# The second convolution's first DFT step: through DRAM instead of SBUF, with the jobs, the load buffers and the moves regrouped

## Chip, cores and metric

One core of a Trainium2 chip. The metric is the device time of one execution in microseconds (us); the median of several runs counts.

## What is computed

One layer of a diffusion trunk on 2048 tokens of width 1024: a modulated norm, a Hyena long convolution of order 2, a residual norm, and an expert-choice mixture of 16 SwiGLU experts. The change lies in the long convolution alone. The reference, cut to it:

```python
def _hyena(h, w_in, b_in, conv_w, conv_b, ..., f_bias, w_out, b_out):
    u = _centred_conv3(h @ w_in + b_in, conv_w, conv_b)
    v, x1, x2 = jnp.split(u, 3, -1)
    kf = _hyena_filters(L, ...)                 # rfft of two filters per channel
    def long_conv(zin, o):
        zf = zin.astype(F32)
        y = jnp.fft.irfft(jnp.fft.rfft(zf, n=2 * L, axis=1) * kf[None, :, o], n=2 * L, axis=1)[:, :L]
        return (y + zf * f_bias[o].astype(F32)).astype(h.dtype)
    z = x1 * long_conv(v, 0)
    z = x2 * long_conv(z, 1)
    return z @ w_out + b_out
```

So there are two long convolutions in a row per channel. The gated result of the first (order 0) is the input of the second (order 1).

## The kernel before

`phase_conv` does both convolutions. The 1024 channels are cut into four channel blocks `cb` of 256, and a *job* is one channel block and one order `o`: eight jobs, in the order cb 0 and 1 with o = 0, cb 0 and 1 with o = 1, then the same for cb 2 and 3. I number them 0 to 7; "a second-order job" is one with o = 1.

A transform of 4096 points is done as two DFT steps, both matmuls with constant matrices. The result of the first step for the first product (`ud`), and the transformed filters after their first step (`fud`), were written to DRAM by earlier stages. A job runs over 16 groups `gp`. For each group it

- loads a filter tile `kr` (from `fud`) and an input tile `xr`; a tile of 512 KB covers two groups (`fetch_k` L825, `fetch` L815 and L819);
- does the second DFT step of both on PE into `xp` (`spec` L833, `fwd` L853), copies the filter's spectrum with ACT, and multiplies the spectra on DVE (L858, L859);
- does the first step of the inverse on PE (`inv`, `ap`), copied by ACT to `ao` (L872), and moves it in two DMAs of 128 KB from `ao` into a tile `bn`, which regroups the partitions (`put`, L879).

While job j runs, its groups 2 to 9 also finish job j - 1: `bst` does the inverse's second step on PE from `bn` into `sb`, for order 0 in three passes on operands that `bsplit` split into a high part (ACT, L900) and a low part (POOL, L901); `gate` multiplies by x1 or x2 (DVE, L929). After an order 1 product the gated result goes to DRAM (`zd`, L937). After an order 0 one it is split (ACT L933, POOL L934), and `s1st` does the second product's first DFT step on it at groups 4 to 11: three-pass matmuls into `sb`, copied by ACT (L806) into tiles `s1o` in SBUF. The second-order job two places later gets its `xr` from `s1o`, by DMAs of 128 KB from SBUF to SBUF, two per group.

The order is written out by hand: every engine works off its instructions in the order in which the loop below issues them, and DMAs go out in order from the queue of the engine that issues them. SP issues all loads and the first of the two moves of a group, POOL the second. `ahead` sends `kr` five groups ahead and `xr` four, each with two buffers. `after` starts the next stage's weights (`wod`) during the last job.

Of the kernel before, what the change touches and what calls it, by code (L numbers as in the profile page):

```python
# [12 lines left out]
F32 = mybir.dt.float32  # L13
# [28 lines left out]
AH = 2  # L42
SB = 3
# [70 lines left out]
def host_consts():  # L114
    f4 = np.float32
    S1, S2, A, B = dft_mats()
    c = {}
# [4 lines left out]
    c["c_s1p"] = S1.transpose(1, 0, 2)[:, :, spread]  # L122
# [647 lines left out]
def phase_conv(tc, A, wst, s2, am, fud, ud, x1d, x2d, zd, O, after):  # L770
# [4 lines left out]
    with ExitStack() as st:  # L775
# [6 lines left out]
        so = rst.enter_context(tc.tile_pool(reuse_waits="tile", name="c_so", bufs=3, side="right"))  # L782
# [7 lines left out]
        nc.sync.dma_start(s1, A["c_s1p"])  # L790
# [3 lines left out]
        jobs = [(2 * b2 + b, o) for b2 in range(2) for o in range(2) for b in range(2)]  # L794
        s1o, bn, kk, kr, xr = {}, {}, {}, {}, {}
# [3 lines left out]
        def s1st(j, q):  # L799
            if q == 0:  # L800
                s1o[j] = [so.tile([128, 16, 256], F32, name="s1o") for _ in range(2)]
            zh, zl = zs.pop((j, q))
            for th in range(2):
                p = ps.tile([128, 2, 256], F32, name="sb", bufs=3)
                mm3(nc, p, s1h[:, th], s1l[:, th], zh, zl)
                nc.scalar.copy(s1o[j][th][:, 2 * q:2 * q + 2], p)  # L806

        def fetch(j, gp):
            cb, o = jobs[j]
            th = gp // 8  # L810
            gl = (2 * gp) % 16
            if gp % 2 == 0:
                r = rt.tile([128, 4, 256], F32, name="xr", bufs=2)
                if o == 0:
                    nc.sync.dma_start(r, ud[cb, th, gl:gl + 4].rearrange("g p c -> p g c"))  # L815
                xr[j, gp], xr[j, gp + 1] = r[:, 0:2], r[:, 2:4]
            if o == 1:
                for i in range(2):
                    nc.sync.dma_start(xr[j, gp][:, i], rows8(s1o[j][th], gl + i))  # L819

        def fetch_k(j, gp):
            cb, o = jobs[j]
# [97 lines left out]
        def gate(j, q, p):  # L920
# [9 lines left out]
            if o == 0:  # L930
# [4 lines left out]
                zs[j + 2, q] = zh, zl  # L935
# [5 lines left out]
        def ahead(n):  # L941
            for d, f in ((AH + 3, fetch_k), (AH + 2, fetch), (AH + 1, spec), (AH, fwd)):
                m = n + d
                if 0 <= m < len(order) and (d != AH + 3 or m % 2 == 0):
                    f(*order[m])

        for n in range(-AH - 3, 0):
            ahead(n)
        for n, (j, gp) in enumerate(order):
# [10 lines left out]
            if (j + 1, q) in zs:  # L960
                s1st(j + 1, q)
# [717 lines left out]
def build(tc, A, out):  # L1679
    nc = tc.nc  # L1680
    with ExitStack() as st:
# [3 lines left out]
        ud = dr.tile([4, 2, 16, 128, 256], F32, name="ud")  # L1685
        x1d = dr.tile([4, 128, 16, 256], F32, name="x1d")
# [59 lines left out]
        phase_conv(tc, A, wst, S.s2, S.am, fud, ud, x1d, x2d, zd, O, lambda w4, wk: out_start(tc, A, wst, w4, wk, wod, zd, rowd, O))  # L1746
# [20 lines left out]
```

## Time and profile before

| | |
|---|---|
| time, three runs | 4205.91, 4205.35, 4202.3 us; median 4205.35 |
| the profiled execution | 4207.69 us, span 4205.7 us |
| mean granted PE clock | 0.967 of full |
| busy share of the span | PE 93%, DVE 62%, ACT 45%, POOL 23% |
| the convolution, first to last copy `ao` | 1037.3 to 1610.6 us |

The span is what the profiler's trace covers; the rows further down are from this one execution. Most of the kernel is the expert stage behind the convolution, with PE at 90% and more. The convolution's 573 us are a seventh of the span.

### The profile page before, as it was taken

The page shows a single profiled execution, that of the slowest core. Times are in us where ns is not written, and L with a number is a line of the kernel's source. Part 1 is how long each engine was busy: PE and PEld are TensorE (multiplying, and loading weights), DVE is VectorE, ACT ScalarE, POOL GpSimd, SP SyncE. Part 2 cuts the span into 40 slices and gives each one's busy share as a digit, 9 for nine tenths or more (in the row PEclk, how much of TensorE's full clock was granted, in tenths as well). Part 3 has the DMA queues.
Part 4 walks back from the last instruction along what each step waited for, and adds up shares of the span by engine and source line. Part 5 has one row for each costly group of instructions (what it writes and reads, how often), then busy time and mean ns, then how long its engine had stood idle before and what let it go on. Part 6 is the DMA issues. An engine that isn't in the chain of part 4 may idle for free.

```text
span 4205.7 us, 59336 instructions
## 1 busy us (share of the span) xinstructions
PE 3916.2 (93%) x23158; PEld 3360.2 (80%) x23158; DVE 2623.2 (62%) x3636; ACT 1886.3 (45%) x2609; POOL 961.1 (23%) x918
## 2 busy tenths in 40 slices
PE   6788999999998987965999999999999999999997
PEld 2445787787777776755999999999999999998996
DVE  7997444776766766876555555555555555556666
ACT  4554332334876873122444444444444444444443
POOL 4674211222332342120000000000000000005635
PEclk7999999999999999987999999999999999999999
DMA  6665445666778776543566666666566656656664
GB/s 188 189 203 177 129 153 174 206 212 194 208 208 230 208 222 205 166 165 123 189 213 201 191 190 201 200 191 201 192 209 194 204 193 209 193 171 228 225 230 166
DMA packets 648180, 815.30 MB, mean 194 GB/s; under 512 B 51411, under 2 KB 543203, under 8 KB 645596
## 3 DMA queue, kind: packets, MB, share of 16 engines
q1 hardware_dynamic: 593442, 694.82, 52.3%
q0 software_dynamic: 37472, 113.86, 9.3%
q10 hardware_dynamic: 16986, 2.83, 0.4%
q8 instruction: 182, 2.98, 0.3%
q14 instruction: 98, 0.80, 0.1%
HBM read 627.04 MB, written 133.97 MB: 181 GB/s over the span
## 4 chain that ended last, share of the span: by engine, by line
PE 74%; DVE 10%; DMA 8%; issue 4%; POOL 3%; ACT 1%; SPq 0%; POOLq 0%; DVEq 0%; ACTq 0%
PE ab L175 10%; PE ab L177 10%; PE ab L176 10%; PE acc L175 5%; PE acc L176 5%; PE acc L177 5%; PE ip L175 4%; PE ip L177 4%; PE ip L176 4%; DMA xr<-s1o 3%; PE xp L853 1%; PE op L175 1%; PE op L177 1%; PE op L176 1%; PE xp L833 1%
## 5 line engine op out<-in xcount | busy, mean ns | idle before, releaser
L177 PE MATMUL ab<-xh,w1l 128*128 128x256 f32 x2048 | 581.5, 284 | 3.2 <-DVE w1l L1386 3.0
L175 PE MATMUL ab<-xh,w1h 128*128 128x256 f32 x2048 | 582.9, 285 | 0.0
L177 PE MATMUL ab<-xh,w3l 128*128 128x256 f32 x2048 | 579.7, 283 | 0.5 <-DVE w3l L1386 0.5
L176 PE MATMUL ab<-xl,w1h 128*128 128x256 f32 x2048 | 579.8, 283 | 0.0
L176 PE MATMUL ab<-xl,w3h 128*128 128x256 f32 x2048 | 579.6, 283 | 0.0
L175 PE MATMUL ab<-xh,w3h 128*128 128x256 f32 x2048 | 579.6, 283 | 0.0
L1386 DVE TENSOR_TENSOR w2l<-w2r,w2h 128x2048 fp32r<-128x2048 f32 x126 | 297.6, 2362 | 317.6 <-ACT w2h L1385 317.6
L175 PE MATMUL acc<-w2h,hh 128*128 128x512 f32 x1024 | 405.4, 396 | 14.0 <-ACT hh L170 13.5
L176 PE MATMUL acc<-w2l,hh 128*128 128x512 f32 x1024 | 403.3, 394 | 0.0
L177 PE MATMUL acc<-w2h,hl 128*128 128x512 f32 x1024 | 400.5, 391 | 0.8 <-DVE hl L171 0.8
L175 PEld LDWEIGHTS ab<-xh,w1h 128*128 128x128 f32 x2048 | 392.5, 192 | 8.8 <-ACT xh L1469 0.3
L176 PEld LDWEIGHTS ab<-xl,w1h 128*128 128x128 f32 x2048 | 392.4, 192 | 8.6
L177 PEld LDWEIGHTS ab<-xh,w1l 128*128 128x128 f32 x2048 | 392.2, 191 | 4.2 <-DVE w1l L1386 4.2
L177 PEld LDWEIGHTS ab<-xh,w3l 128*128 128x128 f32 x2048 | 393.2, 192 | 0.9 <-DVE w3l L1386 0.9
L176 PEld LDWEIGHTS ab<-xl,w3h 128*128 128x128 f32 x2048 | 393.2, 192 | 0.0
L175 PEld LDWEIGHTS ab<-xh,w3h 128*128 128x128 f32 x2048 | 393.1, 192 | 0.0
L1492 DVE TENSOR_TENSOR s<-s,ab 128x256 f32<-128x256 f32 x256 | 106.9, 417 | 399.6 <-ACT s L1491 399.5
L1386 DVE TENSOR_TENSOR w1l<-w1r,w1h 128x2048 fp32r<-128x2048 f32 x126 | 301.0, 2389 | 69.5 <-ACT w1h L1385 69.4
L1386 DVE TENSOR_TENSOR w3l<-w3r,w3h 128x2048 fp32r<-128x2048 f32 x126 | 292.9, 2325 | 53.8 <-ACT w3h L1385 53.8
L1515 POOL DMA_INDIRECT accd<-y,idx x27 | 64.4, 2385 | 1120.2 <-DVE y L1509 1120.2
L1385 ACT CAST w2h<-w2r 128x2048 fp32r<-128x2048 f32 x128 | 244.0, 1906 | 153.3 <-PE acc L177 145.1
L1491 ACT ACTIVATE s<-ab 128x256 f32<-128x256 f32 x256 | 97.4, 380 | 448.0 <-PE ab L177 448.0
(401 smaller groups left out, 8728.1 us busy)
## 6 DMA issues: line engine op xcount, KB each, us to landing
w1r<-in_moe_w_dram SPq DMA_DIRECT2D x128, 1024.0 KB
w3r<-in_moe_w_dram SPq DMA_DIRECT2D x128, 1024.0 KB
w2r<-in_moe_w_dram SPq DMA_DIRECT2D x128, 1024.0 KB
fud<-ev SPq DMA_DIRECT2D x128, 256.0 KB
kr<-fud SPq DMA_DIRECT2D x64, 512.0 KB
mw<-in_mod_w_dram SPq DMA_DIRECT2D x96, 256.0 KB
wraw<-in_hy_w_in_dram SPq DMA_DIRECT2D x48, 512.0 KB
win<-in_c_win_dram SPq DMA_DIRECT2D x64, 256.0 KB
```

The source lines that it names most:

```text
L175: nc.tensor.matmul(out, lhsT=ah, rhs=bh, start=start, stop=False)
L176: nc.tensor.matmul(out, lhsT=ah, rhs=bl, start=False, stop=False)
L177: nc.tensor.matmul(out, lhsT=al, rhs=bh, start=False, stop=stop)
L833: nc.tensor.matmul(p[:, i], lhsT=s2[:, 2 * gp + i], rhs=r[:, i], start=True, stop=True)
L853: nc.tensor.matmul(p[:, i], lhsT=s2[:, 2 * gp + i], rhs=r[:, i], start=True, stop=True)
L1385: nc.scalar.copy(h, raw)
L1386: eng.tensor_tensor(l, raw, f_(h), OP.subtract)
L1491: nc.scalar.activation(s, p[:, 0], AF.Silu)
L1492: nc.vector.tensor_tensor(s, s, p[:, 1], OP.mult)
L1515: nc.gpsimd.indirect_dma_start(out=accd, out_offset=at(idx, h), in_=y, in_offset=None, compute_op=OP.add)
```

## The change

The jobs run in the order o = 0 for all four channel blocks, then o = 1 for all four. The first DFT step's result is copied by ACT into a small tile `s1t` (three buffers of 256 KB) instead of `s1o`, and written from there to a new DRAM tile `z1d`, in the layout of `ud`, by a DMA on POOL's queue. A second-order job loads `xr` from `z1d` as a first-order one does from `ud`: one DMA of 512 KB for two groups. `kr` and `xr` have four buffers each and are sent eight to nine groups ahead. Both moves of a group go on POOL's queue (those of the last four groups on SP's and ACT's). Even jobs' second `bn` tile has a place of its own, `bn2`. The constant of the first step is no longer permuted (`c_s1` for `c_s1p`).

```diff
-        so = rst.enter_context(tc.tile_pool(reuse_waits="tile", name="c_so", bufs=3, side="right"))
...
-        jobs = [(2 * b2 + b, o) for b2 in range(2) for o in range(2) for b in range(2)]
+        jobs = [(cb, o) for o in range(2) for cb in range(4)]
...
         def s1st(j, q):
-            if q == 0:
-                s1o[j] = [so.tile([128, 16, 256], F32, name="s1o") for _ in range(2)]
             zh, zl = zs.pop((j, q))
             for th in range(2):
                 p = ps.tile([128, 2, 256], F32, name="sb", bufs=3)
                 mm3(nc, p, s1h[:, th], s1l[:, th], zh, zl)
-                nc.scalar.copy(s1o[j][th][:, 2 * q:2 * q + 2], p)
+                t = rt.tile([128, 2, 256], F32, name="s1t", bufs=3)
+                nc.scalar.copy(t, p)
+                nc.gpsimd.dma_start(z1d[jobs[j][0], th].rearrange("g (s n) c -> (g s) n c", s=8)[:, 2 * q:2 * q + 2], t)

         def fetch(j, gp):
             cb, o = jobs[j]
-            th = gp // 8
             gl = (2 * gp) % 16
-            if gp % 2 == 0:
-                r = rt.tile([128, 4, 256], F32, name="xr", bufs=2)
-                if o == 0:
-                    nc.sync.dma_start(r, ud[cb, th, gl:gl + 4].rearrange("g p c -> p g c"))
-                xr[j, gp], xr[j, gp + 1] = r[:, 0:2], r[:, 2:4]
-            if o == 1:
-                for i in range(2):
-                    nc.sync.dma_start(xr[j, gp][:, i], rows8(s1o[j][th], gl + i))
+            r = rt.tile([128, 4, 256], F32, name="xr", bufs=XR)
+            nc.sync.dma_start(r, (ud, z1d)[o][cb, gp // 8, gl:gl + 4].rearrange("g p c -> p g c"))
+            xr[j, gp], xr[j, gp + 1] = r[:, 0:2], r[:, 2:4]
...
-            r = rt.tile([128, 4, 256], F32, name="kr", bufs=2)
+            r = rt.tile([128, 4, 256], F32, name="kr", bufs=XR)
...
-                bn.setdefault(j, []).append(wk.tile([128, 16, 256], F32, name="bn", bufs=3))
+                own = th and j % 2 == 0
+                bn.setdefault(j, []).append((rt if own else wk).tile([128, 16, 256], F32, name="bn2" if own else "bn", bufs=1 if own else 3))
...
-                (nc.sync, late and nc.scalar or nc.gpsimd)[i].dma_start(rows8(bn[j][gp // 8], gl), ao[:, i])
+                (late and (nc.sync, nc.scalar)[i] or nc.gpsimd).dma_start(rows8(bn[j][gp // 8], gl), ao[:, i])
...
-                zs[j + 2, q] = zh, zl
+                zs[j + 4, q] = zh, zl
...
-            for d, f in ((AH + 3, fetch_k), (AH + 2, fetch), (AH + 1, spec), (AH, fwd)):
+            for d, f in ((AH + 2 * XR - 1, fetch_k), (AH + 2 * XR - 2, fetch), (AH + 1, spec), (AH, fwd)):
                 m = n + d
-                if 0 <= m < len(order) and (d != AH + 3 or m % 2 == 0):
+                if 0 <= m < len(order) and (d < AH + 2 or m % 2 == 0):
                     f(*order[m])
...
-            if (j + 1, q) in zs:
-                s1st(j + 1, q)
+            if (j + 3, q) in zs:
+                s1st(j + 3, q)
```

POOL's order in job 1, at the last group without and the first with a split and a first DFT step, before:

```order
L934 TENSOR_TENSOR w<-z,w 128x512
L879 DMA bn<-ao 8x16x256
L934 TENSOR_TENSOR w<-z,w 128x512
L901 TENSOR_TENSOR w<-bn,w 128x512 x2
L879 DMA bn<-ao 8x16x256
```

The full groups after the change (`bn_8886` is `bn2`):

```order
L929 TENSOR_TENSOR w<-z,w 128x512
L896 TENSOR_TENSOR w<-bn,w 128x512
L896 TENSOR_TENSOR w<-bn_8886,w 128x512
L806 DMA z1d<-s1t 128x512 x2
L874 DMA bn<-ao 8x16x256 x2
L929 TENSOR_TENSOR w<-z,w 128x512
```

A group's round on POOL now holds two writes to `z1d` and two moves where it held one move; they stand between the splits of one group and the low part (L929) of the next.

SP's order where the first second-order job's loads go out, before:

```order
L825 DMA kr<-fud 128x4x256
L879 DMA bn<-ao 8x16x256
L819 DMA xr<-s1o 128x1x256 x2
L879 DMA bn<-ao 8x16x256
L825 DMA kr<-fud 128x4x256
L819 DMA xr<-s1o 128x1x256 x2
```

And after:

```order
L880 DMA x<-x1d 128x1024
L812 DMA xr<-ud 128x4x256
L819 DMA kr<-fud 128x4x256
L812 DMA xr<-z1d 128x4x256
L819 DMA kr<-fud 128x4x256
```

The moves and the loads from `s1o` are gone from SP; what is left are loads from DRAM.

ACT's order after the change, one such group, with what each instruction waits for (`DMASW` are the landings of DMAs on POOL's queue):

```order
L928 CAST w<-z 128x512 [waits DVE_49]
L829 COPY k<-xp 64x512 [waits PE_49]
L830 COPY k<-xp 64x512
L831 COPY k<-xp 64x512
L832 ACTIVATE k<-xp 64x512
L895 CAST w<-bn 128x512 [waits PE_49,Pool_49]
L895 CAST w<-bn_8886 128x512 [waits PE_49,Pool_49]
L805 COPY s1t<-sb 128x512 [waits DMASW3_49,PE_49]
L805 COPY s1t<-sb 128x512 [waits DMASW6_49,PE_49,Activation_49]
L867 COPY ao<-ap 128x512 [waits DMASW5_49,DMASW4_49,PE_49]
```

The copies into `s1t` (L805) now wait for a landing, each for that of the write three copies back, and the copy `ao` (L867) waits for two landings on POOL's queue.

## Rows read from the trace of the kernel before

**Rows 1.** The page, part 4: the chain that ended last, by engine and line
```profile
PE ab L175 10%; PE ab L177 10%; PE ab L176 10%; PE acc L175 5%; PE acc L176 5%; PE acc L177 5%; PE ip L175 4%; PE ip L177 4%; PE ip L176 4%; DMA xr<-s1o 3%; PE xp L853 1%; PE op L175 1%; PE op L177 1%; PE op L176 1%; PE xp L833 1%
```

**Rows 2.** Windows, job by job: start:end us, busy us (instructions), PEclk, DMA share, GB/s
```profile
1037.30:1087.30 50.00, 44.75 (x191) 34.32 (x189) 46.08 (x69) 45.36 (x82) 9.63 (x16) 1.00 0.95 237
1087.30:1160.00 72.70, 67.72 (x282) 53.81 (x282) 49.22 (x76) 62.49 (x114) 33.64 (x34) 0.98 0.70 192
...
1234.20:1309.90 75.70, 64.10 (x320) 52.22 (x320) 50.15 (x76) 46.39 (x81) 15.67 (x24) 0.93 0.85 232
...
1529.50:1610.60 81.10, 58.89 (x290) 46.42 (x291) 42.66 (x64) 37.57 (x65) 17.68 (x27) 0.88 0.82 240
sum 573.30, PE 505.23 PEld 404.53 DVE 390.39 ACT 426.09 POOL 193.58; mean PE 63.15 PEld 50.57 DVE 48.80 ACT 53.26 POOL 24.20
```

**Rows 3.** Waits of PE in the convolution: us in total, times, longest us
```profile
PE xp L853 <- DMA xr<-s1o: 30.1, 23, 10.2
PE xp L833 <- DMA kr<-fud: 23.4, 15, 2.7
PE xp L853 <- DMA xr<-ud: 11.4, 7, 3.3
```

**Rows 4.** The critical chain inside job 3: start us, us, what
```profile
1238.17 9.75 DMA xr<-s1o
...
1247.94 9.92 DMA xr<-s1o
```

**Rows 5.** Waits of SP's queue in the convolution: us in total, times, longest us
```profile
SPq L879 <- ACT ao L872: 94.7, 50, 6.7
SPq L879 <- ACT w L933: 60.8, 20, 6.4
```

**Rows 6.** POOL's timeline in job 1: start us, us, instruction, idle before it
```profile
1114.42 2.89 POOL L901 TENSOR_TENSOR w<-bn,w 128x512 fp32r<-128x512 f32 x2 [0.94 <-ACT w L900]
1117.25 0.61 POOL L879 DMA_DIRECT2D bn<-ao  x1
1117.88 1.30 POOL L934 TENSOR_TENSOR w<-z,w 128x512 fp32r<-128x512 f32 x1
1119.81 2.87 POOL L901 TENSOR_TENSOR w<-bn,w 128x512 fp32r<-128x512 f32 x2 [0.63 <-ACT w L900]
```

**Rows 7.** POOL's timeline in job 0, plain groups
```profile
1041.12 0.60 POOL L879 DMA_DIRECT2D bn<-ao  x1 [2.22 <-ACT ao L872]
1044.02 0.60 POOL L879 DMA_DIRECT2D bn<-ao  x1 [2.29 <-ACT ao L872]
```

**Rows 8.** POOL's timeline in job 3, groups with a second-order predecessor
```profile
1253.80 0.74 POOL L937 DMA_DIRECT2D zd<-z  x1 [3.09 <-DVE z L929]
...
1258.18 0.74 POOL L937 DMA_DIRECT2D zd<-z  x1 [3.01 <-DVE z L929]
```

**Rows 9.** Windows: loads kr, xr alone (1026 to 1030) and job 0's later part
```profile
1026.00:1030.00 4.00, 1.89 (x8) 1.17 (x7) 3.86 (x7) 3.88 (x8) 0.87 (x2) 0.98 1.08 362
...
1058.00:1087.00 29.00, 24.19 (x104) 18.79 (x103) 25.76 (x40) 24.92 (x45) 5.37 (x9) 1.00 0.98 242
```

**Rows 10.** DMA issues of the convolution: count, KB each, median us to landing
```profile
kr<-fud SPq DMA_DIRECT2D x60, 512.0 KB
...
bn<-ao POOLq DMA_DIRECT2D x124, 128.0 KB, 6.3
```

**Rows 11.** Writes ud<-vt before the convolution, line L609: issue ns min/median/max
```profile
L609 POOL DMA_DIRECT2D ud<-vt x80: 706/750/943, 404.2 to 995.8; - x80
...
DMA to landing us min/median/max: 2.2/3.4/6.0
```

**Rows 12.** Tile ao: how long its moves take to land
```profile
DMA to landing us min/median/max: 2.8/6.3/9.5
```

**Rows 13.** SP's timeline at the start of the convolution
```profile
1019.65 0.46 SPq L825 DMA_DIRECT2D kr<-fud  x1
1024.06 0.38 SPq L815 DMA_DIRECT2D xr<-ud  x1
```

More of the change, by code (lines that the diff above doesn't have):

```diff
@@ L42 @@
 AH = 2
+XR = 4
 SB = 3
@@ L121, in host_consts @@
     spread = np.array([8 * (4 * (p // 32) + p % 4) + p // 4 % 8 for p in range(128)])
-    c["c_s1p"] = S1.transpose(1, 0, 2)[:, :, spread]
     c["c_b"] = B.transpose(1, 0, 2)[spread]
@@ L767, in phase_in, with phase_conv @@
             pass
-def phase_conv(tc, A, wst, s2, am, fud, ud, x1d, x2d, zd, O, after):
+def phase_conv(tc, A, wst, s2, am, fud, ud, x1d, x2d, z1d, zd, O, after):
     nc = tc.nc
@@ L789, in phase_conv @@
         s1 = wk.tile([128, 2, 128], F32, name="ao", bufs=3)
-        nc.sync.dma_start(s1, A["c_s1p"])
+        nc.sync.dma_start(s1, A["c_s1"])
         split_const(nc, s1h, s1, s1l)
@@ L793, in phase_conv @@
         split_const(nc, bmh, bm, bml)
-        jobs = [(2 * b2 + b, o) for b2 in range(2) for o in range(2) for b in range(2)]
-        s1o, bn, kk, kr, xr = {}, {}, {}, {}, {}
+        jobs = [(cb, o) for o in range(2) for cb in range(4)]
+        bn, kk, kr, xr = {}, {}, {}, {}
         zs = {}
         def s1st(j, q):
-            if q == 0:
-                s1o[j] = [so.tile([128, 16, 256], F32, name="s1o") for _ in range(2)]
             zh, zl = zs.pop((j, q))
@@ L941, in ahead @@
         def ahead(n):
-            for d, f in ((AH + 3, fetch_k), (AH + 2, fetch), (AH + 1, spec), (AH, fwd)):
+            for d, f in ((AH + 2 * XR - 1, fetch_k), (AH + 2 * XR - 2, fetch), (AH + 1, spec), (AH, fwd)):
                 m = n + d
-                if 0 <= m < len(order) and (d != AH + 3 or m % 2 == 0):
+                if 0 <= m < len(order) and (d < AH + 2 or m % 2 == 0):
                     f(*order[m])
-        for n in range(-AH - 3, 0):
+        for n in range(1 - AH - 2 * XR, 0):
             ahead(n)
@@ L1685, in build @@
         ud = dr.tile([4, 2, 16, 128, 256], F32, name="ud")
+        z1d = dr.tile([4, 2, 16, 128, 256], F32, name="z1d")
         x1d = dr.tile([4, 128, 16, 256], F32, name="x1d")
@@ L1744, in moe @@
             yield from moe_start(tc, A, wst, R)
-        phase_conv(tc, A, wst, S.s2, S.am, fud, ud, x1d, x2d, zd, O, lambda w4, wk: out_start(tc, A, wst, w4, wk, wod, zd, rowd, O))
+        phase_conv(tc, A, wst, S.s2, S.am, fud, ud, x1d, x2d, z1d, zd, O, lambda w4, wk: out_start(tc, A, wst, w4, wk, wod, zd, rowd, O))
         R.split_first = phase_out(tc, A, S.x16, rowd, ident, O, accd, xnd, lg, moe)
```

## The prediction

> **What bounds the kernel now.** I read first the chain that ended last, on the page: most of it is matmuls of the experts, which the change doesn't touch, but 3% of the span, by far the largest entry that isn't a matmul, is the DMA xr<-s1o [rows 1]. Next the stretches, one for each of the eight jobs of the convolution (cut at each job's first copy of the inverse's result): 573.3 us in all, 50 to 81 us each [rows 2]. Two things are to be seen there. Jobs that split their predecessor's result (job 1; jobs 2, 5 and 6 are like it) keep PE busy for 67.7 of 72.7 us with DMA at 0.70. Jobs after a second-order one (job 3; 4 and 7 are like it) have PE at 64.1 of 75.7 or 58.9 of 81.1 us, DMA at 0.82 to 0.85 and a lower granted clock, 0.93 and 0.88. Then who PE waited for: the three loads alone, 30.1 + 23.4 + 11.4 = 64.9 us [rows 3]. In the chain inside job 3 one xr<-s1o follows the other, 9.8 us each with nothing between [rows 4]: with two buffers the next load of a buffer is sent only when the last is used, so a pair of groups can't be quicker than one such DMA. SP, which sends them, also stands 94.7 us before moves bn<-ao until ACT has made ao, and 60.8 us before others; all loads behind stand with it [rows 5].
>
> What the engines alone would take per group, from unstalled stretches: 2.90 us for a plain group (two moves, 1041.12 and 1044.02) [rows 7]; 4.38 us with a second-order predecessor's inverse step (1253.80 to 1258.18) [rows 8]; 5.39 us with split and first step (1114.42 to 1119.81) [rows 6]. Job 0 has 16 plain groups: 46.4 us. Job 1 has 6 plain, 2 + 2 with one of the two steps (I take 4.38 for each) and 6 full: 17.4 + 17.5 + 32.3 = 67.2. Job 3 has 8 of 2.90 and 8 of 4.38: 58.2.
>
> **What the DMA engines would take.** While kr and xr alone are loaded the 16 engines move 362 GB/s at a share of 1.08, which is 335 at 1, or 2.98 us per MB. In job 0's full stretch, a third each of kr, xr and moves bn<-ao, it is 242 GB/s at 0.98, or 4.05 us per MB [rows 9]. So a move inside SBUF costs 3 x 4.05 - 2 x 2.98 = 6.2 us per MB. A job loads 8 kr and 8 xr of 512 KB, 4.19 MB each, and moves 32 times 128 KB, 4.19 MB [rows 10]. With this price job 3 needs 12.5 (kr) + 26 (s1o) + 26 (moves) + 6.3 (x2d, 2.1 MB) + 6.3 (zd, 2.1 MB) = 77 us against its measured 75.7: it is at its DMA floor, and its serial loads are how that shows.
>
> Here a rule speaks against the change. The Trainium skill (DMA: Bandwidth & Descriptors, Where 436 GB/s comes from) lets HBM transfers be bound at about 358 GB/s and SBUF to SBUF ones at 435. An estimate from that page makes a move cost 2.3 us per MB and a load 2.8; sending s1o through DRAM would then add 4.19 x (2 x 2.8 - 2.3) = 14 us of DMA time per channel block, 55 us in all, and job 3 would need 43 us, so that DMA would bound nothing and the time would be rival 1's. The trace disagrees (242 beside 362), and the sum goes by the trace.
>
> **The change, part by part.**
> (a) Jobs in the order o = 0 four times, then o = 1 four times. Before, jobs 1, 2, 5 and 6 had a first-order predecessor and 3, 4, 7 a second-order one; now they are 1 to 4 and 5 to 7. The number of matmuls is the same. Nothing to pay by itself.
> (b) xr<-s1o (128 DMAs, two per group) goes; xr<-z1d comes, one 512 KB load for two groups, and 64 writes z1d<-s1t of 256 KB, 4.19 MB in each of jobs 1 to 4. DMA time: a second-order job gives back 4.19 x (6.2 - 3.0) = 13.4 us; a first-order one's result costs 12.5 us to write. How dear a write is the stage doesn't show: bounds 2.98 (load) and 6.2 us per MB (move); I take 2.98, since a write touches SBUF once.
> (c) Four buffers for kr and xr, sent up to eight groups ahead: about 23 us of plain groups, against the 9 to 10 us of a load. What PE waits for then is bandwidth, not one DMA's time. DMA floors: job 0 12.5 + 12.5 + 26 = 51 us; jobs 1 to 4 add 6.3 (x) and 12.5 (z1d): 69.8; jobs 5 to 7 add 6.3 + 6.3: 63.5. Before, by the same prices, all eight and the change's total come out within 1%: the DMA work isn't less, it is spread evenly and may run ahead.
> (d) All moves on POOL's queue, 4 in place of 2 transfers per full group. POOL does, in order: zl 1.30, two splits 2.88, two z1d, two moves at 0.61 [rows 6]. The issue of z1d isn't in the trace: nearest is ud<-vt, also 256 KB, same arrangement, 0.71 to 0.94, median 0.75 us [rows 11]; I take 0.75 (by the bounds 6.8 to 7.3 us in all). 1.30 + 2.88 + 1.50 + 1.22 = 6.90 us, against 5.39 of ACT and PE now, when POOL still idles 0.63 us before the splits. So POOL is the bound in groups 4 to 8 of jobs 1 to 4. Queued behind a late issue are the next zl and the splits, for which PE's next inverse step waits. The first of the five shifts only what stands behind its splits, four pay 1.5 us: 6 us per job. SP is then never held by ao; its queue has only loads.
> (e) s1t has three buffers, so ACT's second copy of a group waits until z1d of the group before has landed. Over two groups this asks 5.4 + D + L, where D is z1d's delay behind the splits (about 1.7 us) and L its landing; ud<-vt takes 2.2 to 6.0, median 3.4 [rows 11], moves on POOL 2.8 to 9.5, median 6.3 [rows 12]. With L = 5: 6.0 per group, below 6.90, so hidden in groups 5 to 8; in groups 10 and 11, (4.4 + 5) / 2 = 4.7 against 4.4: 0.6 us per job, of which I make 1.
> (f) bn2 gives a fourth bn; before, a move could wait until the split had used one up. SP no longer sends them, and POOL's order has the splits ahead of the moves: nothing. The permuted constant is another of the same size: nothing.
> (g) The first kr now lies where the projection's last weights are, and waits for its last matmuls: it leaves at 1024 and not 1019.65, like the first xr [rows 13]. PE's first job starts about 3 us later (0 to 4.4).
>
> **Sum.** Each job takes its largest floor. Job 0: 51. Jobs 1 to 4: 67.2 + 6 + 1 = 74.2, over the DMA's 69.8, four times 297. Jobs 5 to 7: 63.5, three times 190.5. The last job ends at a copy, one group less: -2.9. wod's 1024 x 1024 numbers (4.2 MB, 12.5 us) fall where the loads have stopped eight groups early (8 x 0.52 MB, 12.5 us): 0. Together 535.6 for 573.3, -37.7; start +3: **-34.7 us**. The profiled execution took 4207.69 us, its span 4205.7; the median of the three runs is 4205.35. 4205.35 - 34.7 = **4171 us**.
>
> **Rivals.**
> 1. *Moves were dear because they use few of the engines, and POOL spreads them.* For it: job 3 is bound by DMA at a share of 0.85, not 1. Against: job 0 reaches 0.98 with the same dear moves. Then DMA is no bound: 46.4 + 297 + 3 x 58.2 - 2.9 = 515, -58 + 3: 4150 us. The Trainium skill (same page, Why a DMA increments its semaphore by 16 and not by 1) gives such a rule: a transfer with 8 rows on one side runs on 8 engines, always the lowest 8 from SP, a rotating 8 from POOL; no row names the engines. Chance 0.25.
> 2. *The change gives nothing: the writes cost like moves.* Jobs 1 to 4 need 69.8 + 13.4 = 83 us of DMA: 51 + 333 + 190.5 - 2.9 = 571, +3: about 4206 us. For it: a DMA share of 0.98 was reached already without them. Against: the ud writes before the stage land in 2.2 to 6.0 us [rows 11]. Chance 0.17.
> 3. *Slower: ACT waits for z1d.* At L = 9.5, the slowest move of the stage, groups 5 to 9 take (5.4 + 1.7 + 9.5) / 2 = 8.3 in place of about 6.6, groups 10 and 11 7.0: 13 us more per job, 51 in all, 4222 us. It decides from L of about 7.9 on, where the 34.7 us are gone. For it: moves take up to 9.5 in this stage [rows 12]. Against: in jobs 1 to 4 as they are, DMA is at 0.70, and their slower groups spread the load. Chance 0.10.
>
> **How the numbers follow.** The forecast keeps 0.48. A measurement of this kernel tells about 0.2% (8.4 us) from no change: 4197 to 4214. Rival 1 and nearly all of the forecast are faster, so are 0.4 of rival 2 and a little of rival 3: 0.79. Slower: 0.7 of rival 3 and a fifth of rival 2, 0.10; same 0.11. The range reaches down into rival 1 (POOL's loss remains there) and up to rival 2's edge: 4135 to 4204, leaving out the low third of rival 1 and rival 3 with half of rival 2. The likeliest case alone: 4155 to 4190 (start 0 to 4.4, z1d issue, DMA price by 5%).
>
> **What would show it.** Right: no PE wait on xr in the second half; PE waits for kr and xr together under 25 us; jobs 5 to 7 at 60 to 66 us with DMA over 0.9; in groups 5 to 9 of jobs 1 to 4 POOL without idle time at 6.9 us a group and PE waiting for the splits; jobs 1 to 4 no quicker than before. Wrong: jobs 1 to 4 at 67 (POOL hidden), s1t's copies held by z1d, or jobs 5 to 7 still over 70.

## The result, and the profile after

The changed kernel takes **4175.71 us** (median of four runs, 4171.36 to 4179.8), the kernel before 4205.63: a ratio of 0.9934, 95% interval 0.992 to 0.9949, or 29.9 us less. The profiled execution took 4177.93 us, its span 4176.1, against 4205.7: 29.6 us less. 4171 was forecast, in a range of 4135 to 4204.

The chain that ended last, by engine and line, on the page of the changed kernel (to be read beside [rows 1]):

```profile
PE ab L175 11%; PE ab L177 11%; PE ab L176 11%; PE acc L175 5%; PE acc L176 5%; PE acc L177 5%; PE ip L175 4%; PE ip L177 4%; PE ip L176 4%; DMA bn<-ao 4%; PE op L175 1%; PE op L177 1%; PE op L176 1%; PE xp L827 1%; PE ap L865 1%
```

xr<-s1o is gone from it; the moves bn<-ao stand there in its place, with 4%. The stretches, cut at each job's first copy ao as in [rows 2]; jobs 0, 1, 3, 5 and the sum:

```profile
1040.50:1090.10 49.60, 45.42 (x192) 34.97 (x192) 45.47 (x69) 45.01 (x81) 19.04 (x32) 1.00 1.10 270
1090.10:1165.30 75.20, 67.86 (x284) 52.24 (x282) 54.66 (x76) 62.69 (x114) 51.39 (x66) 1.00 0.92 256
...
1241.10:1322.20 81.10, 71.92 (x282) 55.88 (x282) 55.34 (x77) 62.91 (x114) 51.32 (x66) 0.94 0.84 233
...
1399.90:1462.20 62.30, 58.51 (x316) 51.03 (x317) 47.04 (x72) 45.84 (x80) 25.07 (x40) 0.97 0.98 264
...
sum 545.00, PE 488.40 PEld 392.86 DVE 407.82 ACT 424.98 POOL 300.89; mean PE 61.05 PEld 49.11 DVE 50.98 ACT 53.12 POOL 37.61
```

The convolution takes 545.0 us for 573.3, and the 28.3 us are a difference of two large numbers. The three jobs that follow a second-order one took 75.7 + 72.4 + 81.1 = 229.2 us before and now 62.3 + 61.6 + 61.7 = 185.6: 43.6 less. The four jobs with a split and a first step took 294.1 and now 75.2 + 75.8 + 81.1 + 77.7 = 309.8: 15.7 more. Job 0 gave 0.4. Of job 3's 81.1 us some 4 belong to TensorE's clock (an estimate): PE's busy time is 71.9 us at a mean granted clock of 0.94, against 67.9 at 1.00 in job 1, so a part of it ran at 1.2 and not 2.4 GHz, after PE had idled at the job's start (busy 1.75 of the 4 us from 1244 on, then a clock of 0.63).

Who PE waited for in the eight jobs (us in total, times, longest), beside [rows 3], the five largest:

```profile
PE ap L865 <- ACT ao L867: 29.7, 29, 7.2
PE sb L904 <- DMA bn<-ao: 7.7, 4, 2.2
PE sb L911 <- DMA bn<-ao: 6.9, 3, 2.4
PE sb L175 <- DVE z L924: 6.6, 4, 1.7
PE sb L176 <- POOL w L896: 4.5, 10, 1.9
```

Not one of the five rows is a load, and the two left out (0.8 us together) aren't either. The 64.9 us of waits for xr and kr are gone; PE now waits for ACT's copy ao, for moves bn<-ao that haven't landed when the next job needs them, and a little for DVE and POOL. Two of ACT's waits in the same stretch say what stands behind the first row:

```profile
ACT ao L867 <- DMA bn<-ao: 29.4, 29, 7.8
...
ACT s1t L805 <- DMA z1d<-s1t: 10.3, 8, 2.7
```

And the issues' table gives the landings (KB each, median us to landing):

```profile
bn<-ao POOLq DMA_DIRECT2D x248, 128.0 KB, 7.2
...
z1d<-s1t POOLq DMA_DIRECT2D x64, 256.0 KB, 4.3
```

The tile ao has three buffers, and a copy waits for the landing of the moves of three groups before, which take 7.2 us in the median from their issue. The first load kr leaves at 1024.74 us, for 1019.65 in [rows 13].

### The profile page after: what moved, and what is told of

It reads as the page before. It is cut to its first block, busy times and chain, and to the rows that moved or that the text cites. A ratio compares the mean times of both kernels' runs of the same rounds, so it can differ in the third digit from the quotient of the medians.

```text
span 4176.1 us, 59155 instructions
## 1 busy us (share of the span) xinstructions
PE 3898.9 (93%) x23158; PEld 3350.6 (80%) x23158; DVE 2639.2 (63%) x3636; ACT 1885.7 (45%) x2609; POOL 1067.4 (26%) x1106
## 3 DMA queue, kind: packets, MB, share of 16 engines
q8 instruction: 182, 2.98, 0.3%
## 4 chain that ended last, share of the span: by engine, by line
PE 74%; DVE 8%; DMA 7%; POOL 4%; issue 3%; ACT 2%; SPq 0%; ACTq 0%; POOLq 0%; DVEq 0%
PE ab L175 11%; PE ab L177 11%; PE ab L176 11%; PE acc L175 5%; PE acc L176 5%; PE acc L177 5%; PE ip L175 4%; PE ip L177 4%; PE ip L176 4%; DMA bn<-ao 4%; PE op L175 1%; PE op L177 1%; PE op L176 1%; PE xp L827 1%; PE ap L865 1%
## 5 line engine op out<-in xcount | busy, mean ns | idle before, releaser
L175 PE MATMUL acc<-w2h,hh 128*128 128x512 f32 x1024 | 404.3, 395 | 13.4 <-ACT hh L170 13.4
```

The lines of the kernel that those rows point to most:

```text
L175: nc.tensor.matmul(out, lhsT=ah, rhs=bh, start=start, stop=False)
```

## Experiments

Each edit is one of the changed kernel unless it says otherwise. Ratios are to the kernel before, with 95% intervals. Job numbers and the cuts are as above. Where a figure is of jobs or groups, it is from the one traced execution of that run. The stretch behind the convolution, where nothing was changed, took 2590.6 us in the changed kernel's trace and up to 2599.1 in the others', so of a difference between whole times some microseconds can lie there.

My theory after the trace, A: loads sent ahead and an SP that doesn't stand are what ended PE's waits, and what jobs 1 to 4 lose is POOL's queue, made longer by z1d and the moves. Its rivals, each explained in the expectation where it comes up: B, the DMA engines' total work is the pace; C, moves are dear when SP's queue sends them; D, one large load from DRAM is the gain; E, moves on SP's queue are late because loads stand ahead of them; F, SP standing before the moves is what held the loads; S, POOL holds DVE.

**1. The writes to z1d on SP's queue.**

```diff
-                nc.gpsimd.dma_start(z1d[jobs[j][0], th]...
+                nc.sync.dma_start(z1d[jobs[j][0], th]...
```

> The writes z1d<-s1t go out from SP's queue instead of POOL's; nothing else differs from the changed kernel. Theory A (in jobs 1 to 4 POOL's round is the pace: low part 1.28, two splits 2.5, two z1d 1.17, two moves 1.25 = 6.2 us against 5.4 of ACT and PE): the full groups fall to 5.4 to 5.6 us, jobs 1 to 4 lose 3 to 6 us each, the time is 4152 to 4165 us. Theory B (the DMA engines' total work, at a share of 0.84 to 0.92 in these jobs, is the pace): the same bytes move, so the time stays within 4 us of the changed kernel's 4175.7.

Measured: 4160.57 us (4155.53 to 4163.49), ratio 0.9899 (0.9883 to 0.9914). Jobs 1 to 4, job 1 and the sum:

```profile
1083.90:1155.50 71.60, 67.20 (x285) 52.78 (x284) 50.35 (x76) 62.57 (x115) 42.75 (x50) 1.00 0.97 265
...
sum 285.50, PE 270.84 PEld 212.36 DVE 199.93 ACT 250.17 POOL 172.02; mean PE 67.71 PEld 53.09 DVE 49.98 ACT 62.54 POOL 43.00
```

285.5 us for 309.8, a little over 6 us per job. Theory A's numbers hold, theory B's fail: as many bytes move, and at a higher DMA share (0.95 to 0.99) than in the changed kernel (0.84 to 0.92). The whole gains less than these jobs' 24.3 us, 15.1 by the medians: jobs 5 to 7 took 3.6 us longer here (189.2 in all, to the last copy), and the stretch behind the convolution 6.7.

**2. The moves alternate between SP and POOL again.**

```diff
-                (late and (nc.sync, nc.scalar)[i] or nc.gpsimd).dma_start(rows8(...
+                (nc.sync, late and nc.scalar or nc.gpsimd)[i].dma_start(rows8(...
```

> The two moves of a group go out one from SP and one from POOL, as in the kernel before; the rest is the changed kernel. Theory A (POOL paces jobs 1 to 4; which queue a move is on does not change what it costs the DMA engines): POOL's round falls to 5.6 us, jobs 1 to 4 lose 2 to 3 us each, jobs 0 and 5 to 7 stay within 1 us, the time is 4163 to 4172 us. Theory C (moves became cheap because POOL's queue spreads them over more engines; job 0's DMA share went from 0.95 to 1.10): job 0 is back at a share of 0.95 to 1.0, jobs 5 to 7 take 65 to 70 us instead of 62, the time is 4182 us or more.

Measured: 4217.54 us (4215.05 to 4224.7), ratio 1.0038 (1.0025 to 1.0052): 42 us more than the changed kernel and slower than the kernel before. Jobs 0, 5, 6 and 7:

```profile
1040.20:1091.50 51.30, 45.87 (x193) 34.88 (x192) 46.55 (x70) 45.04 (x82) 9.66 (x16) 1.00 1.03 263
1417.50:1479.70 62.20, 58.96 (x321) 51.69 (x320) 48.70 (x75) 46.01 (x81) 15.74 (x24) 0.97 0.95 261
1479.70:1547.50 67.80, 60.64 (x326) 52.41 (x324) 53.44 (x80) 45.81 (x80) 16.92 (x26) 0.97 0.95 260
1547.50:1616.00 68.50, 54.86 (x287) 47.51 (x288) 41.59 (x62) 37.40 (x64) 17.72 (x27) 0.89 0.82 242
```

The wait of SP's queue that is the largest in total over the eight jobs:

```profile
SPq L874 <- ACT ao L867: 208.3, 88, 7.1
```

And PE's for the last job's moves:

```profile
PE sb L911 <- DMA bn<-ao: 10.8, 2, 7.1
```

Theory A is refuted here: jobs 1 to 4 took 87.3, 78.4, 76.6 and 83.7 us, though POOL's round is 0.6 us shorter. Theory C's time comes about, but not quite as it was put: job 0's share is 1.03 and not 0.95 to 1.0, job 5 keeps 62.2 us, jobs 6 and 7 lose 6 to 7. In them the middle groups keep their 4.4 us; what is lost stands at the job's second group (9.6 and 12.8 us), where PE waits for the last job's last moves. So it isn't bandwidth over the job, it is how late single moves land. No wait of PE before `xp` is put down to a load in this trace, so it isn't kr and xr held behind a standing SP either. Of the 39.0 us between the two traces 30.8 are in the convolution and 8.5 behind it.

The table of issues has no landing for SP's moves, but the trace's semaphore events do. Of the last pair of moves of jobs 0 to 6, SP's half landed 7.9 to 15.1 us after its issue and POOL's half, issued 0.2 to 0.3 us later, 6.3 to 7.8; each time PE went on within 0.6 us of SP's landing. In the changed kernel both halves are POOL's and landed after 7.7 to 9.0 us.

**3. Two buffers, sent as before.**

```diff
-XR = 4
+XR = 2
...
-            for d, f in ((AH + 2 * XR - 1, fetch_k), (AH + 2 * XR - 2, fetch), ...
+            for d, f in ((AH + 3, fetch_k), (AH + 2, fetch), ...
```

> kr and xr have two buffers each and are sent five and four groups ahead, as in the kernel before; z1d, the order of the jobs and the moves are those of the changed kernel. Theory A (what ended the waits of PE is loads that are sent ahead): loads again come one behind the other, PE waits 20 to 50 us in all for kr and xr, jobs 5 to 7 take 66 to 72 us instead of 62, the time is 4190 to 4205 us. Theory D (one DMA of 512 KB from DRAM in place of two of 128 KB per group inside SBUF is the gain, and the number of buffers is not): jobs 5 to 7 stay at 62 to 64, the time is 4173 to 4182 us.

Measured: 4188.47 us (4187.0 to 4197.34), ratio 0.9965 (0.9952 to 0.9979). PE's waits for loads:

```profile
PE xp L847 <- DMA xr<-z1d: 11.4, 7, 5.5
...
PE xp L827 <- DMA kr<-fud: 3.5, 3, 1.5
...
PE xp L847 <- DMA xr<-ud: 2.6, 2, 1.5
```

And jobs 5 to 7:

```profile
1402.00:1466.70 64.70, 59.80 (x321) 51.37 (x320) 49.78 (x76) 45.93 (x81) 25.07 (x40) 0.97 0.97 259
1466.70:1528.80 62.10, 57.92 (x320) 49.63 (x319) 49.49 (x76) 45.92 (x81) 26.27 (x42) 1.00 1.01 275
1528.80:1601.40 72.60, 54.65 (x287) 46.34 (x285) 44.68 (x66) 37.38 (x65) 24.91 (x39) 0.87 0.95 264
```

This trace is of the slowest of the run's five executions (4197.34 us). In it 17.5 us of waits for loads are back, and jobs 5 to 7 take 199.4 us for 185.6. The four buffers are worth 12.8 us by the medians, 13.8 by these three jobs. Both expectations missed on the time, by 1.5 us and 6.5 us: theory A is the nearer, and more than half of the gain isn't the buffers'. PE's 17.5 us are below theory A's 20 to 50, too.

**4. No writes to z1d.**

```diff
-                nc.gpsimd.dma_start(z1d[jobs[j][0], th]...[:, 2 * q:2 * q + 2], t)
...
-            nc.sync.dma_start(r, (ud, z1d)[o][cb, gp // 8, ...
+            nc.sync.dma_start(r, (ud, ud)[o][cb, gp // 8, ...
```

> Nothing is written to z1d, and second-order jobs load xr from ud instead: the second convolution is left without its right input, all else works as in the changed kernel. It shows what the 64 writes cost by issue, landing and DMA work together. Theory A: jobs 1 to 4 lose POOL's 1.17 us per full group and the waits for landings, 4 to 8 us each, the time is 4146 to 4160 us, about what z_sp gives or up to 6 us less. Theory B (DMA work is the pace, and a write costs 3 to 6 us per MB): jobs 1 to 4 lose 8 us and more each, the time is below 4145 us, and it is 15 us or more below z_sp.

Measured: 4145.17 us (4144.21 to 4146.83), ratio 0.9862 (0.9847 to 0.9877). Jobs 1 to 4, job 1 and the sum:

```profile
1090.00:1158.80 68.80, 65.48 (x280) 52.21 (x279) 49.34 (x75) 62.52 (x114) 43.10 (x50) 1.00 0.79 213
...
sum 274.60, PE 264.20 PEld 210.88 DVE 199.51 ACT 250.58 POOL 172.29; mean PE 66.05 PEld 52.72 DVE 49.88 ACT 62.64 POOL 43.07
```

The writes to z1d are left out here, and the second-order jobs load ud in its place. The time lies between the two expectations: 0.8 us below theory A's range, 0.2 above theory B's mark of 4145. Theory B's other two marks are met: 15.4 us below run 1, where A had said 6 at most and B 15 at least, and 8.8 us less per job than the changed kernel, where B had said 8 and more. Its price isn't: B had a write at 3 to 6 us per MB. Against run 1 the 64 writes, 16.8 MB, cost these jobs 285.5 - 274.6 = 10.9 us, or 0.65 us per MB (0.92 by the medians). With the DMA share down to 0.79 job 1 still takes 68.8 us, within 2 us of the 67.2 that were worked out for ACT and PE. A total that bounds the job would have given back 12.5 us per job by the price of a load (2.98 us per MB); 2.7 were given back, and run 12, with all bytes moved, takes 270.8 us for these jobs, 3.8 less than this run. So what the writes cost is more likely how late other transfers land beside them; that isn't shown directly.

**5. The kernel before, with the moves alone on POOL's queue.**

```diff
-                (nc.sync, late and nc.scalar or nc.gpsimd)[i].dma_start(rows8(...
+                (late and (nc.sync, nc.scalar)[i] or nc.gpsimd).dma_start(rows8(...
```

> The kernel before, with one part of the change alone: both moves of a group on POOL's queue. s1o, the order of the jobs and two buffers stay. Theory A (the loads from s1o come one behind the other with two buffers, whoever sends the moves): jobs 3, 4 and 7 still take 70 to 81 us, jobs 1, 2, 5 and 6 gain what SP's waits cost and lose 0.6 us of POOL per full group, the time is 4195 to 4208 us. Theory F (what the change undid is SP standing before the moves, 94.7 us for ao, and the moves standing among the loads): PE's waits for xr and kr fall by half, the time is 4190 us or less.

Measured: 4189.35 us (4186.46 to 4193.83), ratio 0.9967 (0.9956 to 0.9978): 15.3 us less than before from this line alone. PE's waits for loads, beside [rows 3]:

```profile
PE xp L853 <- DMA xr<-s1o: 29.3, 24, 6.4
PE xp L833 <- DMA kr<-fud: 9.0, 9, 1.6
...
PE xp L853 <- DMA xr<-ud: 3.0, 4, 0.9
```

And jobs 3 and 4:

```profile
1231.30:1303.90 72.60, 64.84 (x324) 53.23 (x323) 50.04 (x76) 46.13 (x80) 25.17 (x40) 0.93 0.92 240
1303.90:1369.80 65.90, 59.16 (x316) 50.04 (x314) 50.44 (x77) 45.88 (x81) 25.15 (x40) 0.97 0.95 258
```

The waits for kr and for xr<-ud fall from 34.8 to 12.0 us, those for xr<-s1o stay (29.3 us for 30.1). The time is theory F's, by 0.65 us: the loads that stood behind SP's waits come earlier, though PE's waits for loads fall by a third and not by half (41.3 us for 64.9). The serial loads from s1o remain, as theory A said, and jobs 3 and 7 still take 72.6 and 80.6 us; job 4 takes 65.9, below theory A's 70.

**6. Alternating moves and two buffers.** The edits of runs 2 and 3 together.

> The changed kernel with alternating moves and with two buffers sent as in the kernel before, both edits together: what is left of the change is z1d, bn2 and the order of the jobs. Moves back on SP alone cost 42 us with four buffers, two buffers alone 13 us. Theory C (moves from SP's queue are dear to the DMA engines in themselves): the costs add, 4225 us or more. Theory E (a move on SP's queue is late because the loads that are sent far ahead, and the loads of x before them, stand ahead of it): with loads sent only as far ahead as before, less stands ahead of a move, and the time is below that with four buffers: 4192 to 4212 us.

Measured: 4211.37 us (4207.12 to 4221.98), ratio 1.002 (1.0009 to 1.0032). The costs of the two edits, 42 and 13 us, don't add: with two buffers alternating costs 23 us (4188.47 to 4211.37), with four 42. That is in theory E's range, at its upper edge; run 10 tests its reason.

**7. Two buffers, and the jobs in the old order.**

```diff
-        jobs = [(cb, o) for o in range(2) for cb in range(4)]
+        jobs = [(2 * b2 + b, o) for b2 in range(2) for o in range(2) for b in range(2)]
...
-                zs[j + 4, q] = zh, zl
+                zs[j + 2, q] = zh, zl
...
-            if (j + 3, q) in zs:
-                s1st(j + 3, q)
+            if (j + 1, q) in zs:
+                s1st(j + 1, q)
```

> The changed kernel with two buffers sent as in the kernel before, and with the jobs in the old order (two channel blocks with o = 0, the same two with o = 1). Beside the run with two buffers in the new order (4188.5 us) it shows what the order of the jobs does by itself. Theory A: nothing, within 6 us of 4188.5; the order only allows loads of z1d to be sent eight groups ahead. Rival: with the old order the load of a second-order job's first xr, four groups ahead, still waits for the landing of the last write to z1d two groups before it on the path, and SP with all loads behind it: 10 us or more above 4188.5.

Measured: 4193.86 us (4188.86 to 4203.34), ratio 0.9976 (0.9965 to 0.9987): 5.4 us above run 3, and the two intervals overlap, so the order by itself is worth little. PE's wait for xr<-z1d is 20.4 us, 9 more than in run 3, which is the rival's wait at a smaller price.

**8. z1d on SP's queue and six tiles ao.** The edit of run 1, and:

```diff
-            ao = wk.tile([128, 2, 256], F32, name="ao", bufs=3)
+            own = j < 7 and gp % 2
+            ao = (rt if own else wk).tile([128, 2, 256], F32, name="aor" if own else "ao", bufs=3)
```

> The writes to z1d on SP's queue, and six tiles ao in place of three until the last job (those of odd groups in a place of their own). With three, ACT waited 24.2 us in all for moves to land before it could use an ao again, and PE 18.2 us for ACT's copies. Theory A (what is left over the engines' pace is the landing of moves): ACT's wait goes, the plain groups of jobs 1 to 7 come to 2.9 us, the time is 4145 to 4156 us. Rival (the DMA engines' work is what is left): the moves land later and PE waits for them at the job's start in place of this, 4157 to 4163 us.

Measured: 4142.74 us (4141.79 to 4145.7), ratio 0.9857 (0.9838 to 0.9876), the lowest median of all: 33 us below the changed kernel, 62 below the one before. ACT's wait for moves in run 1:

```profile
ACT ao L867 <- DMA bn<-ao: 24.2, 26, 7.6
```

In this run:

```profile
ACT ao L868 <- DMA bn<-ao: 10.6, 2, 7.8
```

And jobs 1 to 4, job 1 and the sum:

```profile
1080.70:1150.30 69.60, 66.94 (x284) 52.80 (x282) 49.76 (x75) 62.51 (x115) 42.72 (x50) 1.00 0.98 269
...
sum 278.00, PE 267.24 PEld 210.97 DVE 199.90 ACT 250.30 POOL 171.95; mean PE 66.81 PEld 52.74 DVE 49.98 ACT 62.57 POOL 42.99
```

The 24.2 us have become 10.6, of which 7.8 are one wait; jobs 1 to 4 come to 278.0 us, 7.5 below run 1. Theory A, and by a little more than it had said.

**9. DVE's add with one operand in PSUM.** In the changed kernel's groups 5 and 6 one thing looked like the whole cause. POOL's timeline in job 1 (start us, us, instruction):

```profile
1112.17 1.29 POOL L929 TENSOR_TENSOR w<-z,w 128x512 fp32r<-128x512 f32 x1
1113.43 2.49 POOL L896 TENSOR_TENSOR w<-bn,w 128x512 fp32r<-128x512 f32 x2
1115.87 1.17 POOL L806 DMA_DIRECT2D z1d<-s1t  x2
1117.03 1.25 POOL L874 DMA_DIRECT2D bn<-ao  x2
1118.29 1.30 POOL L929 TENSOR_TENSOR w<-z,w 128x512 fp32r<-128x512 f32 x1
```

And DVE's:

```profile
1106.73 0.69 DVE L854 TENSOR_TENSOR pz<-pz,qz 128x512 f32<-128x512 f32 x1
...
1112.44 4.03 DVE L854 TENSOR_TENSOR pz<-pz,qz 128x512 f32<-128x512 f32 x1
```

DVE's add of 0.69 us takes 4.03 from 1112.44 on, while POOL works on its low part and two splits without a gap until 1115.9, and the next gate and PE's first split matmul wait for it. It happens once in each of jobs 1 to 4, and a hold of 1.6 to 1.9 us once more in each. The Trainium skill (SBUF — State Buffer, SBUF: two separate sides) says that DVE and GpSimd share one port pair, and that a DVE operation with two inputs in SBUF and a GpSimd one that reads SBUF exclude each other for a whole instruction. The trace agrees, and more: the add stood through three of POOL's instructions. The edit takes one input out of SBUF:

```diff
-            nc.vector.tensor_tensor(z, p, k1, OP.mult)
-            nc.vector.tensor_tensor(z, z, q, OP.add)
+            nc.vector.tensor_tensor(p, p, k1, OP.mult)
+            nc.vector.tensor_tensor(z, p, q, OP.add)
```

> The changed kernel; only the second of DVE's two pz operations reads its first operand from PSUM in place of SBUF (the product is written back into xp). In the changed kernel this add, 0.69 us elsewhere, took 4.0 us once in each of jobs 1 to 4, from the start of a run of POOL's tensor operations (low part, two splits without a gap) to its end; all 128 adds together took 19 us more than 0.69 each. Theory S (what a late POOL costs is that DVE's add, with both operands in SBUF, is held until POOL pauses): the adds are back at 0.7 to 0.8 us, groups 5 and 6 of jobs 1 to 4 fall from 8.0 and 7.4 us, the time is 4158 to 4170 us. Theory A as I first put it (POOL's own round of 6.2 us is the pace): PE waits for the splits in place of DVE, the five full groups keep their sum of 31 us, the time is 4172 to 4180 us.

Measured: 4179.38 us (4173.45 to 4181.26), ratio 0.9933 (0.992 to 0.9947): no gain. All 128 adds in the changed kernel (ns min/median/max, first and last start us):

```profile
L854 DVE TENSOR_TENSOR pz<-pz,qz x128: 691/692/4084, 1036.4 to 1575.9; 128x512 f32<-128x512 f32 x128
```

And in this one:

```profile
L854 DVE TENSOR_TENSOR pz<-xp,qz x128: 690/692/694, 1033.5 to 1573.7; 128x512 f32<-128x512 f32 x128
```

The longest add is 694 ns for 4084, the hold is gone. And yet: the copies ao of six groups of job 1 that bound the five full ones, first and last start, in the changed kernel:

```profile
L867 ACT COPY ao<-ap x6: 591/603/605, 1108.7 to 1139.4; 128x512 f32<-128x512 f32 x6
```

In this one:

```profile
L867 ACT COPY ao<-ap x6: 592/606/606, 1107.1 to 1137.9; 128x512 f32<-128x512 f32 x6
```

And in run 1:

```profile
L867 ACT COPY ao<-ap x6: 586/603/605, 1102.6 to 1129.4; 128x512 f32<-128x512 f32 x6
```

Five groups take 30.7, 30.8 and 26.8 us. Without the hold they are no quicker; group 5 then takes 9 to 10 us by itself, and ACT waits for landings of z1d. Over jobs 1 to 4 it waits 17.0 us for them, against 10.3 in the changed kernel:

```profile
ACT s1t L805 <- DMA z1d<-s1t: 17.0, 8, 4.1
```

So theory S falls: the hold was seen plainly and cost nothing that would not have been lost anyway. 5 x 6.2 = 31 us of POOL's round is what the groups take, and in them POOL is idle for 1.3 us in the changed kernel and 1.3 in this run.

**10. Alternating moves, with kr and xr loaded from POOL's queue.**

```diff
-            nc.sync.dma_start(r, (ud, z1d)[o]...     and     nc.sync.dma_start(r, fud[cb, o, ...
+            nc.gpsimd.dma_start(r, (ud, z1d)[o]...   and     nc.gpsimd.dma_start(r, fud[cb, o, ...
...
-            for d, f in ((AH + 2 * XR - 1, fetch_k), (AH + 2 * XR - 2, fetch), ...
+            for d, f in ((AH + 2 * XR - 3, fetch_k), (AH + 2 * XR - 4, fetch), ...
```

and the moves as in run 2.

> The run with alternating moves (4217.5 us), but with kr and xr loaded from POOL's queue, sent six to seven groups ahead, so that on SP's queue only the loads of x stand among the moves. POOL's queue in jobs 1 to 4 is as long as in the changed kernel or longer, so jobs 0 and 5 to 7 are to be read. Theory C (moves from SP's queue are dear in themselves): jobs 5, 6 and 7 take 62, 68 and 69 us as with alternating moves. Theory E (they are late because kr and xr stand ahead of them): jobs 5 to 7 take 60 to 64 us each, and ACT's waits for moves fall below the 34.7 us of that run.

Measured: 4251.03 us (4248.84 to 4251.85), ratio 1.0105 (1.009 to 1.0121). ACT's waits for moves over the eight jobs:

```profile
ACT ao L867 <- DMA bn<-ao: 53.0, 33, 3.6
```

And PE's:

```profile
PE sb L911 <- DMA bn<-ao: 20.1, 3, 8.9
PE sb L904 <- DMA bn<-ao: 18.0, 3, 6.6
```

Jobs 5 to 7 take 71.5, 69.9 and 70.0 us, again with 4.4 us in the middle groups and 10.8 to 12.3 us in the second. Theory E fails: with only x's loads beside them the moves on SP's queue are no better off. The other half of the moves now stood behind kr and xr on POOL's queue, but that half isn't what PE waited for: of the last pair of jobs 0 to 6, SP's half landed 12.6 to 15.1 us after its issue and POOL's, issued 0.3 us later, 6.4 to 8.8 (from the trace's semaphore events, as in run 2), and PE went on within 0.6 us of SP's landing each time. That speaks for theory C, for these moves: at a job's end a move from SP's queue lands later than its twin from POOL's. A share of x's loads in it isn't excluded. Over all groups the medians hardly differ (6.5 us from SP, 6.8 from POOL; 7.6 and 6.7 in run 2); it is the slowest ones that do (15.1 and 11.3; 15.1 and 10.6).

**11 and 12. The moves in the same group; and the add of run 9 with it.** Run 8 with `LAG = 0` for `LAG = 1`, and the same with the edit of run 9.

> As the run with z1d on SP and six ao (4142.7 us), and each group's moves are sent in the same group, not one group later. Theory A (in group 2 of a job PE waits for the landing of the last job's last moves; that group takes 5 to 7.6 us): the moves land 3 to 5 us earlier, that group falls by 1.5 to 3 us in seven jobs, the time is 4122 to 4134 us. Rival: POOL now stands until ACT has made ao before it can do the next low part, so the full groups grow by half a microsecond or more: 4140 to 4155 us.

> As the run before in this list (z1d on SP, six ao, moves in the same group) and the pz add with one operand in PSUM. Theory S: where POOL isn't late DVE's add is not held (1 us in all with z1d on SP), so this gives within 4 us of the run without it. Rival (POOL's and DVE's tensor operations hold each other in every full group): 8 us or more below it.

Measured: 4146.29 us (4144.81 to 4148.42), ratio 0.9855 (0.984 to 0.987), and 4144.44 (4140.67 to 4145.85), ratio 0.9851 (0.9837 to 0.9864). Neither can be told from run 8: the medians are 3.6 and 1.7 us above it, the ratios a little below. The rival's time holds for the first, but not its reason: jobs 1 to 4 are 275.8 us, 2 below run 8; the second group of jobs 2 to 7 stays at 5.3 to 8.9 us, and job 7 is 4.4 us longer (67.3 for 62.9). What theory S said of the second holds; its jobs 1 to 4 are 270.8 us.

## Why the prediction was right, step by step

The time is 4.7 us above the forecast and inside the likeliest case's own range. That is partly luck. The convolution was to be 37.7 us shorter and is 28.3: jobs 1 to 4 took 12.8 us more than forecast, jobs 5 to 7 2.0 less (185.6 for 190.5 - 2.9) and job 0 1.4 less, and these two for a wrong reason. Another 4.5 us went behind the convolution, where nothing was changed; without them the time would be 9.2 us above the forecast.

- **What bounds the kernel: serial loads of xr and a held SP.** Right. The waits are gone (0 for 64.9 us), and each half shows by itself: moves off SP's queue -15.3 us (run 5), four buffers -12.8 (run 3). With the 0.9 us between these two runs, which differ by z1d, the order of the jobs, bn2 and the constant, that is the 28.9 us from the kernel before to the changed one. Both rows of [rows 5] are waits before moves (L879), 155.5 us in all, and not 94.7 and others.
- **(b), the way through DRAM.** Forecast as 13.4 us of DMA time given back per second-order job. What z1d and the order of the jobs give by themselves is next to nothing: the kernel before with POOL's moves takes 4189.35, the changed kernel with two buffers 4188.47. In the traces, the three jobs behind a second-order one gain 19.7 us (219.1 in run 5, 199.4 in run 3), and the four with a split and a first step, where z1d is written, lose 22.8 (286.2 and 309.0). A write costs 0.65 to 0.92 us per MB of the jobs' time, under both bounds that were given for the DMA engines' (2.98 and 6.2). What the edit does beyond this is to free s1o's place, which the further buffers of kr and xr take, and to bring an order in which loads can run ahead. More buffers beside s1o weren't tried.
- **(c), the DMA floors.** The step that failed. Jobs 5 to 7 were to take 63.5 us each as their floor and took 61.9 in the mean, but not because of it: their middle groups run at the engines' 4.4 and 2.9 us, and what is over 58.2 is the second group (4.2 to 7.4 us) and the stage's end. Job 0 moved 270 GB/s for 49.6 us, 13.4 MB; by 4.05 us per MB it would have needed 54. Its share is 1.10, so a share of 0.98 wasn't full, as the 1.08 of the loads alone in [rows 9] already said, and the price of 6.2 us per MB for a move, worked out from 0.98, was too high. It takes the loads sent ahead to get there: with two buffers job 0 stays at 243 GB/s and 0.97 (run 3). The Trainium skill (DMA: Bandwidth & Descriptors, Where 436 GB/s comes from) has 435 GB/s as the bound of transfers inside SBUF; an estimate from it, 2.3 us per MB for a move, lets DMA's total bound no job. On this the runs agree with it and not with my price: run 12 moves in 270.8 us, in jobs 1 to 4, what my floors gave 279.2 (4 x 69.8). The time that went with it, rival 1's, didn't come, for the reasons below.
- **(d), POOL's round.** In kind right, and in its sum: 6.9 us were forecast per full group and 6.2 measured (z1d 0.59 each, not 0.75; the splits 2.5, not 2.88), 6 us per job were forecast as its price, and taking the writes away from POOL gives 6.1 (run 1: 24.3 in four jobs). Not all of that is where it was forecast: the five full groups of job 1 give 3.9 of it (30.7 and 26.8). How it comes about is not just the round: in run 2 the round is 5.6 us and the five groups of job 1 take 32.3. Whether the issues, or the copies s1t that wait for writes sent late, are the larger part is open; more buffers for s1t would tell, and weren't tried.
- **(d), the other side: moves off SP.** It was costed as POOL's loss alone, with a sentence that SP is free and no price on it. It is the largest single gain: 15.3 us in the kernel before, 23 with two buffers, 42 with four. It is two things. In run 5 loads come earlier (PE's waits for them fall by 23.6 us); in runs 2 and 10 no load is waited for before `xp`, and what is lost is SP's moves that land late. On the second rival 1 was in the right in effect; that the reason is more engines isn't shown.
- **What was left out: the moves' landing.** The tile ao with three buffers was taken as costing nothing. ACT waited 29.4 us for moves to land; six buffers give 17.8 us (run 8 against run 1). In jobs 1 to 4 that is 7.5 us, and the clock in job 3 some 4: together 11.5 of the 12.8 us by which these jobs missed 297. That they add up so in the changed kernel is an estimate; six tiles ao were tried only with z1d on SP.
- **(e)**: 1 us per job was forecast for ACT's waits for z1d; it waited 10.3 us in four jobs, 2.6 each. **(g)**: the first kr left at 1024.74, as forecast (1024), and the first copy came 3.2 us later in this pair of traces; the same place lies between 1032 and 1045 us in the other runs, so 3 us can't be told from chance. The rest of the difference, 29.6 - 28.3 + 3.2 = 4.5 us, lies behind the convolution, where nothing was changed; that stretch scatters too (2590.6 us here, 2597.3 in run 1).
- **Rivals.** 2 (writes as dear as moves) is refuted by run 4. 3 (ACT waits for z1d) exists, at 10.3 us; z1d's landing is 4.3 us in the median, far from where rival 3 would decide (by its own figures from L of about 8.3, not 7.9).

## What to carry to other kernels

Before a term is called a floor of the DMA engines, look for a stretch in which the same transfers run faster: a busy share near 1 was not full here, and taking bytes away (run 4) showed what they cost. When a queue is relieved, price the relief as well as the new queue's burden: the line that moved the DMAs off SP gave most, and the burden on POOL went when the new writes were put on the queue that had become free. A wait that a profile shows plainly (DVE's 4 us) can be a place where lost time shows and not its cause; only taking it away tells. And where two transfers of a pair go out on two queues, ask which of them lands last before you blame what stands ahead of either.

## What the runs showed of the hardware

The same moves of 128 KB are worth 15 to 42 us more or less by the queue that sends them. Two things differ with the queue in the traces. One is the packets. Queue q1 is SP's and q0 POOL's; packets, MB, and the packets' time as a share of 16 engines' span, in the kernel before:

```profile
q1 hardware_dynamic: 593442, 694.82, 52.3%
q0 software_dynamic: 37472, 113.86, 9.3%
```

And in run 5, where 124 moves have gone from SP to POOL:

```profile
q1 hardware_dynamic: 576578, 678.56, 51.2%
q0 software_dynamic: 47392, 130.19, 11.0%
```

That is 136 packets per move less on q1 and 80 more on q0. The data are in packets of 1 KB from SP and of 4 KB from POOL, by the trace's records. The shares add up to 61.6% of 4205.7 us before and 62.2% of 4187.9 us here, so the gain isn't that the engines are busy for less time.

The other is the engines. A move from SP raises its semaphore once about 1 us after its issue and eight times as it lands, a move from POOL sixteen times. The Trainium skill (DMA: Bandwidth & Descriptors, Why a DMA increments its semaphore by 16 and not by 1) says that a transfer gets the largest number of engines up to 16 that divides the slowest dimension of both its sides, which is 8 for one with 8 rows on one side. The eight rises of SP's moves agree; POOL's sixteen don't tell. That SP's are always the same 8 isn't shown here, since the records don't name the engine, and why SP's slowest moves land at 15.1 us where POOL's land at 11.3 (run 10) stays open. The other thing not expected was the hold of DVE's add through three instructions of POOL (run 9).
